# The feed-forward's hidden layer transposed as two planes of 16-bit words by a DMA instead of by TensorE

## The chip, the cores and the metric

The kernel runs on one core of a Trainium2 chip. The metric is the device time of one execution in microseconds; the kernel before takes 300.09 us (median of three runs, 300.06 to 302.69).

## The reference

One decoder layer over 256 tokens of width 1024, in float32: attention with 8 heads of 128, then a SwiGLU feed-forward of width 2816, each behind an RMS norm and with a residual add, and a last RMS norm. With 256 tokens there is one attention block, so the attention is plain causal attention. The part that the change touches is this:

```
def swiglu(h, w_in, w_out):
    g, u = jnp.split(jnp.einsum('bsd,df->bsf', h, w_in), 2, axis=-1)
    return jnp.einsum('bsf,fd->bsd', jax.nn.silu(g) * u, w_out)
```

## The kernel before, in words

All matrix products are made to nearly full float32 accuracy from three passes: a matrix is split into `hi` (cast to the format fp32r by ScalarE) and `lo` (what is left, by a subtract on VectorE), and `mm` (L93) issues hi x hi, hi x lo and lo x hi into one PSUM accumulator. So each 1 MB piece of weights that SP loads into a `raw` tile (four buffers) costs ScalarE a cast (L85) and VectorE a subtract (L86) per half, into `hi` and `lo` tiles (four buffers each).

The order on each engine comes from the Tile framework: it places instructions by its own priorities, keeps what depends on each other in order, and adds the waits. Buffers of a pool are reused in turn, so an instruction that writes a tile waits until the last reader of that buffer is done.

The feed-forward starts at L321. Its hidden layer is made in eleven chunks `c` of 256 hidden columns (gate and value, so 512 columns of `w_in`, in two pieces of 1 MB). `hidden(c)` issues 48 matmuls with 512 columns for the two tiles `t` of 128 tokens, then for each `t` a Silu on ScalarE (L348, tile `sg`) and a product on VectorE (L350), which leaves the chunk in `hs`, tokens on the partitions. The product with `w_out` needs the hidden index on the partitions. This turning is `turn(c)`: four TensorE transposes of 128x128 float32 against an identity into the PSUM tile `ph` (L366), and the split of `ph` into hi and lo by `split` (L354), which go to the large tiles named first, second and third. It is called for chunk c-1 after `hidden(c)`, so that TensorE meets the transposes between two chunks.

For the chunks in `SEVEN` (0, 2, 4, 6, 8) the 2x2 product of blocks with `w_out` is made with seven block products in place of eight. They need four sums of the blocks of `ph` (L377 to L380, tile `fs`) and sums of the rows of `w_out` (`load_out`, L390). To add two blocks that both lie in PSUM, one half of `ph` is first copied to the tile `fc` (L375).

The output stage then goes through the chunks 0 to 8: 21 matmuls for a chunk of SEVEN, 24 for another one. The last two chunks are kept for the end, where each output tile is finished, normed and stored. The turn of chunk 9 stands at the border of the two stages, and that of chunk 10 after the first chunk of the output stage:

```
            if c in SEVEN:
                seven_mm(c, wu[c])
                if c == 0:
                    turn(NC - 1, ph_last)
```

Of the kernel before, what the change touches and what calls it, by code (L numbers as in the profile page):

```python
# [25 lines left out]

F32 = mybir.dt.float32
F32R = mybir.dt.float32r
AF = mybir.ActivationFunctionType
ALU = mybir.AluOpType  # L30
AX = mybir.AxisListType

P = 128
T = 256
NT = T // P
# [5 lines left out]
NC = F // 256  # L41
# [7 lines left out]
SEVEN = (0, 2, 4, 6, 8)  # L49
# [5 lines left out]
def trunk(ctx, tc, xT, x, g2, g3, wv, wqk, wo, w_in, w_out, out):  # L55
    nc = tc.nc
# [8 lines left out]
    def held(n, dtype, slot):  # L65
        return home.tile([P, SLOTS[slot]], dtype, name=slot)[:, :n]

    wpool = ctx.enter_context(tc.tile_pool(name="wpool", bufs=4))
    small = ctx.enter_context(tc.tile_pool(name="small", bufs=2))
    ps_mm = ctx.enter_context(tc.tile_pool(name="ps_mm", bufs=4, space=PSUM))  # L70
    ps_a = ctx.enter_context(tc.tile_pool(name="ps_a", bufs=2, space=PSUM))
    ps_b = ctx.enter_context(tc.tile_pool(name="ps_b", bufs=2, space=PSUM))

    def weights():
        return [wpool.tile([P, 2048], d, name=n) for d, n in ((F32, "raw"), (F32R, "hi"), (F32R, "lo"))]

    def fetch(tiles, src, a, b, pieces=1, queue=nc.sync):

        raw, hi, lo = (w[:, a:b] for w in tiles)
        if queue is not None:  # L80
            queue.dma_start(raw, src[:, a:b])
        n = (b - a) // pieces
        for i in range(0, b - a, n):
            s = slice(i, i + n)
            nc.scalar.copy(hi[:, s], raw[:, s])  # L85
            nc.vector.tensor_sub(lo[:, s], raw[:, s], hi[:, s].bitcast(F32))  # L86

    def load(src, pieces=2):
        tiles = weights()
        fetch(tiles, src, 0, 2048, pieces)  # L90
        return tiles[1:]

    def mm(o, lh, ll, rh, rl, first, last):  # L93
        nc.tensor.matmul(o, lhsT=lh, rhs=rh, start=first, stop=False)  # L94
        nc.tensor.matmul(o, lhsT=lh, rhs=rl, start=False, stop=False)  # L95
        nc.tensor.matmul(o, lhsT=ll, rhs=rh, start=False, stop=last)  # L96
# [3 lines left out]
    ident = const.tile([P, P], F32, name="ident")  # L100
# [16 lines left out]
    nc.vector.memset(eps, EPS)  # L117
    nc.scalar.activation(scr[:, :1], eps, AF.Sqrt)
    pz = ps_b.tile([P, 512], F32, name="pb")
# [10 lines left out]
    def rstd_of(ss, name, bias=eps):  # L130
        r = small.tile([P, 1], F32, name=name)
        nc.scalar.activation(r, ss, AF.Sqrt, bias=bias, scale=1.0 / D)
        nc.vector.reciprocal(r, r)
        return r

    with tc.tile_pool(name="attn2", bufs=2) as a2:
        xh = const.tile([P, KD, T], F32R, name="xh")
        xl = const.tile([P, KD, T], F32R, name="xl")
        oh, ol = held(2 * H * T, F32R, "first").rearrange("p (i h t) -> i p h t", i=2, h=H)

# [6 lines left out]
        for k in range(KD):  # L147
# [5 lines left out]
            else:  # L153
                nc.scalar.activation(xh[:, k], xT_sb[:, k, :T], AF.Copy, scale=g)
            nc.vector.scalar_tensor_tensor(
# [10 lines left out]
            elif k - XK - 1 in range(NT):  # L166

                ss = small.tile([P, 1], F32, name="ss1")
                nc.scalar.activation(scr, x_sb[:, k - XK - 1], AF.Square, accum_out=ss)
                r1.append(rstd_of(ss, f"r1_{k}"))  # L170
        wk = {h: load(wqk[h]) for h in range(2)}

        pv = [[ps_mm.tile([P, 512], F32, name="pmm") for _ in range(2)] for _ in range(NT)]
# [13 lines left out]

        vh, vl = held(2 * D, F32R, "second").rearrange("p (i d) -> i p d", i=2)
        pr = ps_b.tile([P, T], F32, name="pb")
# [3 lines left out]
        for n in range(2):  # L193
            ns = slice(n * 512, (n + 1) * 512)
            nc.scalar.activation(vh[:, ns], pv[0][n], AF.Copy, scale=r1[0])
            nc.vector.scalar_tensor_tensor(
                vl[:, ns], pv[0][n], r1[0], vh[:, ns].bitcast(F32), op0=ALU.mult, op1=ALU.subtract
            )
            nc.scalar.activation(v1[:, ns], pv[1][n], AF.Copy, scale=r1[1])

        qk, pn, pt = {}, {}, {}

        def project(h):
# [10 lines left out]
            )  # L214
            fh = a2.tile([P, 3 * P], F32R, name="qkh")
            fl = a2.tile([P, 3 * P], F32R, name="qkl")
# [78 lines left out]
        r2, xg = [], {}  # L295

        def turn_x1(t, n):
            px = ps_b.tile([P, 4, P], F32, name="pb")
            for j in range(4):
                nc.tensor.transpose(px[:, j], xg[t, n][:, j * P : (j + 1) * P], ident)  # L300
            ks, ts = slice(4 * n, 4 * n + 4), slice(t * P, (t + 1) * P)
            nc.scalar.copy(x1h[:, ks, ts], px)
            nc.vector.tensor_sub(x1l[:, ks, ts], px, x1h[:, ks, ts].bitcast(F32))
# [19 lines left out]
    with tc.tile_pool(name="ffn2", bufs=2) as f2:  # L323
# [7 lines left out]

        hs_ = {}

        def hidden(c):
            u = [load(w_in[2 * c + i]) for i in range(2)]
            pf = [ps_mm.tile([P, 2, 256], F32, name="pmm") for _ in range(NT)]
            order = [(k, t) for k in range(KD) for t in range(NT)]
            if c == 0:
                order.sort(key=lambda kt: kt[1])
            for k, t in order:  # L340
                if c == 0 and (k, t) == (0, 1):
                    turn_x1(1, 1)
                wh, wl = (w.rearrange("p (k n) -> p k n", k=4)[:, k % 4] for w in u[k // 4])
                ts = slice(t * P, (t + 1) * P)
                mm(pf[t].rearrange("p a b -> p (a b)"), x1h[:, k, ts], x1l[:, k, ts], wh, wl, k == 0, k == KD - 1)
            for t in range(NT):
                sg = f2.tile([P, 256], F32, name="sg")
                nc.scalar.activation(sg, pf[t][:, 0], AF.Silu, scale=r2[t])  # L348
                hs_[c, t] = f2.tile([P, 256], F32, name="hs", bufs=4)
                nc.vector.scalar_tensor_tensor(  # L350
                    hs_[c, t], pf[t][:, 1], r2[t], sg, op0=ALU.mult, op1=ALU.mult
                )

        def split(at, src):  # L354

            to = parts(at, at + int(np.prod(src.shape[1:])))
            h, l = (t.rearrange("p (a b) -> p a b", a=src.shape[1]) for t in to)
            nc.scalar.copy(h, src)
            nc.vector.tensor_sub(l, src, h.bitcast(F32))

        def turn(c, ph=None):
            if ph is None:
                ph = ps_a.tile([P, 2, T], F32, name="pa")
            for j in range(2):
                for t in range(NT):
                    nc.tensor.transpose(ph[:, j, t * P : (t + 1) * P], hs_[c, t][:, j * P : (j + 1) * P], ident)  # L366
            if c not in SEVEN:
                split(HAT[c], ph)
                return
            a11, a21, a12, a22 = (ph[:, j, t * P : (t + 1) * P] for j in range(2) for t in range(NT))  # L370
            split(HAT[c], ph[:, 0:1, :P])
            split(HAT[c] + P, ph[:, 1:2])
            fs = f2.tile([P, 4, P], F32, name="fs")
            fc = f2.tile([P, 2, P], F32, name="fc")
            nc.scalar.copy(fc, ph[:, :, P:])  # L375

            nc.vector.tensor_sub(fs[:, 0], a21, fc[:, 1])  # L377
            nc.vector.tensor_add(fs[:, 1], a11, fc[:, 0])
            nc.vector.scalar_tensor_tensor(fs[:, 2], fs[:, 0], -1.0, a11, op0=ALU.mult, op1=ALU.subtract)
            nc.vector.tensor_add(fs[:, 3], a12, fs[:, 2])  # L380
            split(HAT[c] + 3 * P, fs)

        for c in range(NC):
            hidden(c)
            if c > 0:
                turn(c - 1)

# [26 lines left out]
        def bank(pool, n=512):  # L416
            return pool.tile([P, n], F32, name="pmm" if pool is ps_mm else "pb" if pool is ps_b else "pa")


        ph_last = ps_a.tile([P, 2, T], F32, name="pa")  # L420
        acc7 = {i: bank(p) for i, p in ((2, ps_b), (1, ps_b), (3, ps_mm), (7, ps_mm), (5, ps_a), (6, ps_mm), (4, ps_mm))}

        SIDES = {2: (1, 0, 0), 1: (0, 0, 1), 3: (6, 0, 2), 7: (4, 2, 1), 5: (3, 2, 0), 6: (5, 2, 2), 4: (2, 2, 3)}
# [12 lines left out]
                mm(o, *parts(at, at + P), ws[0][:, e], ws[1][:, e], first and j == 0, last and j == 1)  # L436

        TAIL = NC - 2
        wu = {}
        for c in range(TAIL):  # L440
            wu[c] = load_out(c)
            if c in SEVEN:
                seven_mm(c, wu[c])
                if c == 0:
                    turn(NC - 1, ph_last)
                    corners = {(0, 0): acc7[2], (0, 512): acc7[3], (1, 0): acc7[4], (1, 512): bank(ps_a)}
            else:
                for (t, a), o in corners.items():
                    eight_mm(c, wu[c], t, a, 512, o, (t, a) == (1, 512) and c == 1)
        for c in range(TAIL, NC):  # L450
            wu[c] = load_out(c)
# [27 lines left out]
        for i, (t, o, (a, b), (ra, rb)) in enumerate(plan):  # L479
            for c in range(TAIL, NC):  # L480
                eight_mm(c, wu[c], t, a, b - a, o[:, : b - a], o is last and c == TAIL, c == NC - 1)

# [76 lines left out]
```

## Time and profile before

| | |
|---|---|
| median of three runs | 300.09 us (300.06 to 302.69) |
| the profiled execution's own time | 299.56 us |
| span of its trace, first to last instruction | 297.8 us |
| TensorE matmul busy | 290.2 us, 97% |
| VectorE, ScalarE busy | 210.9 us (71%), 167.9 us (56%) |
| transposes of L366 | 44, 272 ns each |
| mean granted TensorE clock | 0.996 |

Matmuls are pipelined: the next one starts before the one ahead has ended, and the ends are modelled. So durations of matmuls cannot be added; the distance from start to start is what one costs on the path. The names PE, PEld, DVE, ACT and SP stand for TensorE, its weight load, VectorE, ScalarE and SyncE; SPq is SP's queue of DMA issues.

### The profile page before, as it was taken

What the parts mean: (1) busy time and instruction counts of PE and PEld (TensorE: products, weight loads), DVE (VectorE), ACT (ScalarE), POOL (GpSimd) and SP (SyncE); (2) the same over time, 40 slices, a digit from 0 to 9 for tenths busy, and PEclk for the clock granted to TensorE, in tenths of its full rate; (3) what the DMA queues carried; (4) which work ended last, traced back from release to release, by engine and by line L of the source; (5) the groups of instructions that cost most, each with busy time, mean ns of one, the idle gap of its engine ahead of it and who ended that gap; (6) DMA issues with size and microseconds to landing.
All of it is one profiled execution on the core that took longest, in us unless ns stands there. A gap on an engine that the chain in (4) does not pass through costs nothing.

```text
span 297.8 us, 4015 instructions
## 1 busy us (share of the span) xinstructions
PE 290.2 (97%) x1544; PEld 247.6 (83%) x1544; DVE 210.9 (71%) x328; ACT 167.9 (56%) x272; POOL 1.3 (0%) x8
## 2 busy tenths in 40 slices
PE   7999999999999999999999999999999999999992
PEld 4788999999988888888888888888888888888881
DVE  4756988777776587657647647749857698888684
ACT  4786886555555496555455446446426647445443
POOL 1000000000000000000000000000000000000000
PEclk9999999999999999999999999999999999999998
DMA  6999895644445406764365465352333444670003
GB/s 200 383 411 418 289 351 194 236 146 151 142 156 190 165 36 222 281 261 155 141 241 183 143 227 196 141 196 88 141 144 119 163 158 145 262 252 31 2 0 141
DMA packets 10099, 55.84 MB, mean 188 GB/s; under 512 B 1120, under 2 KB 2656, under 8 KB 4192
## 3 DMA queue, kind: packets, MB, share of 16 engines
q1 hardware_dynamic: 9648, 55.06, 50.7%
q10 hardware_dynamic: 432, 0.52, 0.5%
q8 instruction: 12, 0.20, 0.3%
q14 instruction: 7, 0.06, 0.1%
HBM read 54.53 MB, written 1.05 MB: 187 GB/s over the span
## 4 chain that ended last, share of the span: by engine, by line
PE 94%; DMA 2%; DVE 1%; ACT 1%; SPq 1%; issue 0%
PE pmm L96 23%; PE pmm L94 23%; PE pmm L95 23%; PE pmm L179 7%; PE pb L96 2%; PE pb L94 2%; PE pb L95 2%; PE pa L94 2%; PE pa L96 2%; PE pa L95 2%; DMA raw<-in_wv 2%; PE pa L366 2%; PE pa L245 1%; PE pb L224 1%; PE pb L260 1%; PE pb L300 1%
## 5 line engine op out<-in xcount | busy, mean ns | idle before, releaser
L86 DVE TENSOR_TENSOR lo<-raw,hi 128x1024 fp32r<-128x1024 f32 (+2 forms) x91 | 106.4, 1185 | 38.9 <-ACT hi L85 38.6
L85 ACT CAST hi<-raw 128x1024 fp32r<-128x1024 f32 (+2 forms) x91 | 90.8, 1021 | 50.1 <-PE pmm L96 23.7
L94 PE MATMUL pmm<-hi,xh 128*128 128x512 f32 x176 | 69.6, 396 | 0.0
L96 PE MATMUL pmm<-hi,xl 128*128 128x512 f32 x176 | 68.7, 390 | 0.0
L95 PE MATMUL pmm<-lo,xh 128*128 128x512 f32 x176 | 68.5, 389 | 0.0
L96 PEld LDWEIGHTS pmm<-hi,xl 128*128 128x128 f32 x176 | 33.0, 188 | 7.1
L95 PEld LDWEIGHTS pmm<-lo,xh 128*128 128x128 f32 x176 | 33.1, 188 | 6.6
L94 PEld LDWEIGHTS pmm<-hi,xh 128*128 128x128 f32 x176 | 33.0, 188 | 6.5
L94 PE MATMUL pmm<-hi,first 128*128 128x512 f32 x76 | 30.3, 398 | 0.0
L95 PE MATMUL pmm<-lo,first 128*128 128x512 f32 x76 | 29.6, 389 | 0.0
L94 PE MATMUL pmm<-xh,hi 128*128 128x256 f32 x96 | 27.6, 287 | 0.0
L96 PE MATMUL pmm<-xh,lo 128*128 128x256 f32 x96 | 27.1, 283 | 0.0
L95 PE MATMUL pmm<-xl,hi 128*128 128x256 f32 x96 | 27.1, 283 | 0.0
L348 ACT ACTIVATE sg<-pmm,r 128x256 f32<-128x256 f32 x22 | 10.4, 475 | 28.8 <-PE pmm L96 28.6
L399 ACT CAST hi<-raw 128x1024 fp32r<-128x1024 f32 (+1 forms) x15 | 17.5, 1193 | 14.9 <-issue 6.6
L400 DVE TENSOR_TENSOR lo<-raw,hi 128x1024 fp32r<-128x1024 f32 (+1 forms) x15 | 20.4, 1398 | 6.2 <-ACT hi L399 6.1
L350 DVE SCALAR_TENSOR_TENSOR hs<-pmm,r,sg 128x256 f32<-128x256 f32 x22 | 10.6, 483 | 14.9 <-ACT sg L348 14.9
L95 PEld LDWEIGHTS pmm<-xl,hi 128*128 128x128 f32 x96 | 18.4, 192 | 0.0
L96 PEld LDWEIGHTS pmm<-xh,lo 128*128 128x128 f32 x96 | 18.4, 191 | 0.0
L94 PEld LDWEIGHTS pmm<-xh,hi 128*128 128x128 f32 x96 | 18.4, 191 | 0.0
L95 PEld LDWEIGHTS pmm<-lo,first 128*128 128x128 f32 x76 | 14.3, 188 | 2.8
L94 PEld LDWEIGHTS pmm<-hi,first 128*128 128x128 f32 x76 | 14.3, 188 | 2.7
(143 smaller groups left out, 425.5 us busy)
## 6 DMA issues: line engine op xcount, KB each, us to landing
raw<-in_w_in SPq DMA_DIRECT2D x22, 1024.0 KB, 4.8
raw<-in_w_out SPq DMA_DIRECT2D x11, 1024.0 KB, 4.8
raw<-in_wqk SPq DMA_DIRECT2D x8, 1024.0 KB, 7.4
raw<-in_wo SPq DMA_DIRECT2D x4, 1024.0 KB, 4.8
raw<-in_wv SPq DMA_DIRECT2D x7, 512.0 KB, 7.7
second<-in_xT SPq DMA_DIRECT2D x8, 128.5 KB, 6.8
x_sb<-in_x SPq DMA_DIRECT2D x1, 1024.0 KB, 9.5
g_bc<-in_g SPq DMA_DIRECT2D x2, 512.0 KB, 5.5
```

Source lines behind the costliest of these rows:

```text
L85: nc.scalar.copy(hi[:, s], raw[:, s])
L86: nc.vector.tensor_sub(lo[:, s], raw[:, s], hi[:, s].bitcast(F32))
L94: nc.tensor.matmul(o, lhsT=lh, rhs=rh, start=first, stop=False)
L95: nc.tensor.matmul(o, lhsT=lh, rhs=rl, start=False, stop=False)
L96: nc.tensor.matmul(o, lhsT=ll, rhs=rh, start=False, stop=last)
L179: nc.tensor.matmul(pv[t][a // 512][:, a % 512 : a % 512 + b - a], lhsT=l[:, k, t * P : (t + 1) * P], rhs=r[:, a:b],  start=k == 0 and a % ...
L224: nc.tensor.matmul(ps[:, :P], lhsT=f[:, :P], rhs=f[:, T : T + P], start=True, stop=True)
L348: nc.scalar.activation(sg, pf[t][:, 0], AF.Silu, scale=r2[t])
L350: nc.vector.scalar_tensor_tensor(hs_[c, t], pf[t][:, 1], r2[t], sg, op0=ALU.mult, op1=ALU.mult)
L366: nc.tensor.transpose(ph[:, j, t * P : (t + 1) * P], hs_[c, t][:, j * P : (j + 1) * P], ident)
L399: nc.scalar.copy(h[:, a:b], r[:, a:b])
L400: nc.vector.tensor_sub(l[:, a:b], r[:, a:b], h[:, a:b].bitcast(F32))
```

## The change

`hs` becomes one tile per chunk, one buffer, with the two 128-column halves, the token tiles and the columns as its axes. `turn(c)` no longer uses TensorE. ScalarE copies `hs`, read as 16-bit words, into a tile `planes`: first all words of one half of the float32 bits, then all of the other (1024 elements in all on a partition). One DMA on SP's queue, `dma_start_transpose`, writes the eight 128x128 blocks of 16-bit words turned into `turned` (two buffers). A new function `join(c)` puts the words together again: a ScalarE copy writes them into `ph`, now a float32 tile in SBUF, and the split and the four sums follow as before, with `ph` as their source. With `ph` in SBUF the copy `fc` goes. `join(c-2)` is called after `turn(c-1)`, so one chunk later than the turn. The loads of `w_in` are now requested one chunk ahead in the program (`early`, `ahead`).

```diff
--- before.py
+++ after.py
@@ -26,6 +26,7 @@
 
 F32 = mybir.dt.float32
 F32R = mybir.dt.float32r
+U16 = mybir.dt.uint16
 AF = mybir.ActivationFunctionType
 ALU = mybir.AluOpType
 AX = mybir.AxisListType
@@ -85,10 +86,17 @@
             nc.scalar.copy(hi[:, s], raw[:, s])
             nc.vector.tensor_sub(lo[:, s], raw[:, s], hi[:, s].bitcast(F32))
 
-    def load(src, pieces=2):
-        tiles = weights()
-        fetch(tiles, src, 0, 2048, pieces)
+    def load(src, pieces=2, raw=None):
+        tiles = [wpool.tile([P, 2048], F32, name="raw") if raw is None else raw]
+        tiles += [wpool.tile([P, 2048], F32R, name=n) for n in ("hi", "lo")]
+        fetch(tiles, src, 0, 2048, pieces, queue=nc.sync if raw is None else None)
         return tiles[1:]
+
+    def early(src):
+
+        raw = wpool.tile([P, 2048], F32, name="raw")
+        nc.sync.dma_start(raw, src)
+        return raw
 
     def mm(o, lh, ll, rh, rl, first, last):
         nc.tensor.matmul(o, lhsT=lh, rhs=rh, start=first, stop=False)
@@ -331,8 +339,10 @@
 
         hs_ = {}
 
+        ahead = {i: early(w_in[i]) for i in range(2)}
+
         def hidden(c):
-            u = [load(w_in[2 * c + i]) for i in range(2)]
+            u = [load(w_in[i], raw=ahead.pop(i)) for i in (2 * c, 2 * c + 1)]
             pf = [ps_mm.tile([P, 2, 256], F32, name="pmm") for _ in range(NT)]
             order = [(k, t) for k in range(KD) for t in range(NT)]
             if c == 0:
@@ -343,12 +353,17 @@
                 wh, wl = (w.rearrange("p (k n) -> p k n", k=4)[:, k % 4] for w in u[k // 4])
                 ts = slice(t * P, (t + 1) * P)
                 mm(pf[t].rearrange("p a b -> p (a b)"), x1h[:, k, ts], x1l[:, k, ts], wh, wl, k == 0, k == KD - 1)
+            hs_[c] = f2.tile([P, 2, NT, P], F32, name="hs", bufs=1)
             for t in range(NT):
                 sg = f2.tile([P, 256], F32, name="sg")
                 nc.scalar.activation(sg, pf[t][:, 0], AF.Silu, scale=r2[t])
-                hs_[c, t] = f2.tile([P, 256], F32, name="hs", bufs=4)
                 nc.vector.scalar_tensor_tensor(
-                    hs_[c, t], pf[t][:, 1], r2[t], sg, op0=ALU.mult, op1=ALU.mult
+                    hs_[c][:, :, t],
+                    pf[t][:, 1].rearrange("p (j f) -> p j f", j=2),
+                    r2[t],
+                    sg.rearrange("p (j f) -> p j f", j=2),
+                    op0=ALU.mult,
+                    op1=ALU.mult,
                 )
 
         def split(at, src):
@@ -358,32 +373,51 @@
             nc.scalar.copy(h, src)
             nc.vector.tensor_sub(l, src, h.bitcast(F32))
 
-        def turn(c, ph=None):
-            if ph is None:
-                ph = ps_a.tile([P, 2, T], F32, name="pa")
-            for j in range(2):
-                for t in range(NT):
-                    nc.tensor.transpose(ph[:, j, t * P : (t + 1) * P], hs_[c, t][:, j * P : (j + 1) * P], ident)
+        turned_ = {}
+
+        def turn(c):
+
+
+            planes = f2.tile([P, 2, 4 * P], U16, name="planes", bufs=1)
+            nc.scalar.copy(planes, hs_[c].bitcast(U16).rearrange("p j t (f w) -> p w (j t f)", w=2))
+            turned = f2.tile([P, 2, 4 * P], U16, name="turned")
+            turned_[c] = turned
+            nc.sync.dma_start_transpose(
+                turned.rearrange("p w (b t) -> p (w b) t", b=4), planes.rearrange("p w n -> p (w n)")
+            )
+
+        def join(c):
+
+            turned = turned_.pop(c)
+            ph = f2.tile([P, 2, T], F32, name="ph", bufs=1)
+
+            tc.keep_in_program_order(
+                nc.scalar.copy(
+                    ph.bitcast(U16).rearrange("p j (t w) -> p (j t) w", w=2), turned.rearrange("p w n -> p n w")
+                )
+            )
             if c not in SEVEN:
                 split(HAT[c], ph)
                 return
             a11, a21, a12, a22 = (ph[:, j, t * P : (t + 1) * P] for j in range(2) for t in range(NT))
             split(HAT[c], ph[:, 0:1, :P])
             split(HAT[c] + P, ph[:, 1:2])
-            fs = f2.tile([P, 4, P], F32, name="fs")
-            fc = f2.tile([P, 2, P], F32, name="fc")
-            nc.scalar.copy(fc, ph[:, :, P:])
-
-            nc.vector.tensor_sub(fs[:, 0], a21, fc[:, 1])
-            nc.vector.tensor_add(fs[:, 1], a11, fc[:, 0])
+            fs = f2.tile([P, 4, P], F32, name="fs", bufs=1)
+
+            nc.vector.tensor_sub(fs[:, 0], a21, a22)
+            nc.vector.tensor_add(fs[:, 1], a11, a21)
             nc.vector.scalar_tensor_tensor(fs[:, 2], fs[:, 0], -1.0, a11, op0=ALU.mult, op1=ALU.subtract)
             nc.vector.tensor_add(fs[:, 3], a12, fs[:, 2])
             split(HAT[c] + 3 * P, fs)
 
         for c in range(NC):
+            for i in range(2 * c + 2, min(2 * c + 4, 2 * NC)):
+                ahead[i] = early(w_in[i])
             hidden(c)
             if c > 0:
                 turn(c - 1)
+            if c > 1:
+                join(c - 2)
 
 
 
@@ -417,7 +451,6 @@
             return pool.tile([P, n], F32, name="pmm" if pool is ps_mm else "pb" if pool is ps_b else "pa")
 
 
-        ph_last = ps_a.tile([P, 2, T], F32, name="pa")
         acc7 = {i: bank(p) for i, p in ((2, ps_b), (1, ps_b), (3, ps_mm), (7, ps_mm), (5, ps_a), (6, ps_mm), (4, ps_mm))}
 
         SIDES = {2: (1, 0, 0), 1: (0, 0, 1), 3: (6, 0, 2), 7: (4, 2, 1), 5: (3, 2, 0), 6: (5, 2, 2), 4: (2, 2, 3)}
@@ -436,15 +469,19 @@
                 mm(o, *parts(at, at + P), ws[0][:, e], ws[1][:, e], first and j == 0, last and j == 1)
 
         TAIL = NC - 2
+        PLAIN = [c for c in range(TAIL) if c not in SEVEN]
         wu = {}
         for c in range(TAIL):
             wu[c] = load_out(c)
             if c in SEVEN:
                 seven_mm(c, wu[c])
                 if c == 0:
-                    turn(NC - 1, ph_last)
+                    turn(NC - 1)
+                    join(NC - 2)
                     corners = {(0, 0): acc7[2], (0, 512): acc7[3], (1, 0): acc7[4], (1, 512): bank(ps_a)}
             else:
+                if c == PLAIN[0]:
+                    join(NC - 1)
                 for (t, a), o in corners.items():
                     eight_mm(c, wu[c], t, a, 512, o, (t, a) == (1, 512) and c == 1)
         for c in range(TAIL, NC):
```

The first place is TensorE between hidden chunks 2 and 3, around the turn of chunk 1. Before:

```order
L95 MATMUL pmm<-lo,xh 128x512
L96 MATMUL pmm<-hi,xl 128x512
L366 MATMUL pa<-ident,hs 128x128 [waits DVE_49] x2
L366 MATMUL pa<-ident,hs 128x128 x2
L94 MATMUL pmm<-hi,xh 128x512 [waits Activation_49]
L95 MATMUL pmm<-lo,xh 128x512
L96 MATMUL pmm<-hi,xl 128x512
```

Now, the same place:

```order
L103 MATMUL pmm<-lo,xh 128x512
L104 MATMUL pmm<-hi,xl 128x512
L102 MATMUL pmm<-hi,xh 128x512 [waits DVE_49]
L103 MATMUL pmm<-lo,xh 128x512
L104 MATMUL pmm<-hi,xl 128x512
```

The four transposes are gone; the matmuls around them stand as they stood (lines 94 to 96 are now 102 to 104). This holds at all eleven places.

The second place is ScalarE's queue from the Silus of chunk 3 to the last cast before those of chunk 4. Before, with the turn of chunk 2:

```order
L348 ACTIVATE sg<-pmm,r_0_1193 128x256 [waits DVE_49,PE_49]
L348 ACTIVATE sg<-pmm,r_1_1239 128x256 [waits DVE_49,PE_49]
L85 CAST hi<-raw 128x1024 [waits DMAHW4_49]
L358 CAST first<-pa 128x128 [waits PE_49]
L85 CAST hi<-raw 128x1024
L358 CAST first<-pa 128x256 [waits DVE_49]
L375 COPY fc<-pa 128x256 [waits DVE_49]
L85 CAST hi<-raw 128x1024 [waits DMAHW5_49,PE_49]
L358 CAST first<-fs 128x512 [waits DVE_49]
L85 CAST hi<-raw 128x1024
```

Now, with the planes of chunk 3 and the join of chunk 2:

```order
L359 ACTIVATE sg<-pmm,r_0_1193 128x256 [waits PE_49]
L359 ACTIVATE sg<-pmm,r_1_1239 128x256 [waits PE_49]
L86 CAST hi<-raw 128x1024 [waits DMAHW6_49]
L382 COPY planes<-hs 128x1024 [waits DMAHW0_49,DVE_49]
L395 COPY ph<-turned 128x1024 [waits Activation_49]
L86 CAST hi<-raw 128x1024
L373 CAST first<-ph 128x128 [waits Activation_49]
L373 CAST first<-ph 128x256
L373 CAST first<-fs 128x512 [waits DVE_49]
L86 CAST hi<-raw 128x1024 [waits DMAHW7_49,PE_49]
L86 CAST hi<-raw 128x1024
```

The two copies stand between the first and the second cast after the Silus. The planes copy waits for the DMA of the chunk before (its semaphore is DMAHW0 here) and for VectorE's product; the join behind it reads what that DMA wrote. The copy fc is gone, and the cast of fs has moved ahead of a weight cast.

The third place is the turnover to the output stage. On SP, before, the loads of `w_out` chunks 1 to 5:

```order
L81 DMA raw<-in_w_out 128x2048 [waits DMAHW5_49,DVE_49]
L396 DMA raw<-in_w_out 128x2048 [waits DMAHW6_49,DVE_49]
L81 DMA raw<-in_w_out 128x2048 [waits DMAHW4_49,DVE_49]
L396 DMA raw<-in_w_out 128x2048 [waits DMAHW0_49,DVE_49]
L81 DMA raw<-in_w_out 128x2048 [waits DMAHW7_49,DVE_49]
```

Now, from the load of chunk 2 to that of chunk 6, with the transposes of hidden chunks 9 and 10 (line 385):

```order
L430 DMA raw<-in_w_out 128x2048 [waits DMAHW5_49,DMAHW2_49,DVE_49]
L385 DMA_TRANSPOSE turned<-planes 128x8x128 [waits DMAHW7_49,Activation_49]
L82 DMA raw<-in_w_out 128x2048 [waits DVE_49]
L430 DMA raw<-in_w_out 128x2048 [waits DMAHW0_49,DVE_49]
L385 DMA_TRANSPOSE turned<-planes 128x8x128 [waits DMAHW6_49,DMAHW1_49,Activation_49]
L82 DMA raw<-in_w_out 128x2048 [waits DVE_49]
L430 DMA raw<-in_w_out 128x2048 [waits DMAHW4_49,DVE_49]
```

On ScalarE now, from the last Silu of the hidden stage to the first casts of `w_out` chunk 4 (L433 with 1536 is the first cast of a seven-product chunk, L86 casts the chunks between):

```order
L359 ACTIVATE sg<-pmm,r_1_1239 128x256 [waits PE_49]
L433 CAST hi<-raw 128x1536 [waits DMAHW2_49]
L382 COPY planes<-hs 128x1024 [waits DMAHW3_49,DVE_49]
L395 COPY ph<-turned 128x1024 [waits Activation_49]
L433 CAST hi<-raw 128x1024 [waits PE_49]
L373 CAST first<-ph 128x512 [waits Activation_49]
L433 CAST hi<-raw 128x1024
L86 CAST hi<-raw 128x1024 [waits DMAHW4_49,PE_49]
L395 COPY ph<-turned 128x1024 [waits DMAHW6_49,DVE_49]
L86 CAST hi<-raw 128x1024
L373 CAST first<-ph 128x512 [waits Activation_49]
L433 CAST hi<-raw 128x1536 [waits DMAHW5_49,PE_49]
```

The transpose of chunk 10 is issued behind the loads of `w_out` chunks 3 and 4. Its join stands in ScalarE's queue between the two casts of chunk 3. Planes and join of the chunks before stand between the casts of chunk 2. On VectorE the wide add of `w_out` chunk 4 (L438, L404 before) now stands ahead of the second subtract of chunk 2; before, it stood behind the subtracts of chunk 3.

## Rows read from the trace of the kernel before

**Rows 1.** The page: busy us of each engine, share of the span, count of instructions.

```profile
PE 290.2 (97%) x1544; PEld 247.6 (83%) x1544; DVE 210.9 (71%) x328; ACT 167.9 (56%) x272; POOL 1.3 (0%) x8
```

**Rows 2.** The page: the chain that ended last, by engine.

```profile
PE 94%; DMA 2%; DVE 1%; ACT 1%; SPq 1%; issue 0%
```

**Rows 3.** Waits of TensorE: us in total, times, longest us.

```profile
PE pb L121 <- DVE eps L117: 1.2, 1, 1.2
PE pmm L179 <- ACT hi L85: 0.5, 2, 0.3
```

**Rows 4.** Line 366: duration ns min/median/max, first and last start us.

```profile
L366 PE MATMUL pa<-ident,hs x44: 272/272/273, 131.9 to 239.8; 128*128 128x128 f32 x44
```

**Rows 5.** The chain in order of time, 154 to 167: start us, us, what.

```profile
154.81 0.44 PE pa L366 x4
...
166.18 0.44 PE pa L366 x4
```

**Rows 6.** Time line, 154 to 168: start us, us, engine, line, operation, tiles.

```profile
154.42 0.39 PE L96 MATMUL pmm<-hi,xl 128*128 128x512 f32 x1
...
154.65 0.60 PE L366 MATMUL pa<-ident,hs 128*128 128x128 f32 x4
...
155.22 1.04 ACT L85 CAST hi<-raw 128x1024 fp32r<-128x1024 f32 x1
155.32 0.40 PE L95 MATMUL pmm<-lo,xh 128*128 128x512 f32 x1
...
155.35 0.48 DVE L350 SCALAR_TENSOR_TENSOR hs<-pmm,r,sg 128x256 f32<-128x256 f32 x1 [0.20 <-ACT sg L348]
...
156.16 0.27 ACT L358 CAST first<-pa 128x128 fp32r<-128x128 f32 x1
...
157.17 0.39 PE L94 MATMUL pmm<-hi,xh 128*128 128x512 f32 x1
...
165.34 0.39 PE L94 MATMUL pmm<-hi,xh 128*128 128x512 f32 x1
```

**Rows 7.** Windows: us, busy us (x instructions) PE, PEld, DVE, ACT, POOL; clock, DMA share, GB/s.

```profile
154.80:166.20 11.40, 11.40 (x55) 9.43 (x53) 7.76 (x14) 6.27 (x10) 0.00 (x0) 1.00 0.51 178
166.20:177.60 11.40, 11.40 (x54) 9.43 (x53) 6.38 (x8) 5.34 (x8) 0.00 (x0) 1.00 0.57 195
```

**Rows 8.** ScalarE, 120 to 234, by line and form: busy us, mean ns; idle before.

```profile
L85 ACT CAST hi<-raw 128x1024 fp32r<-128x1024 f32 x37 | 38.3, 1051 | 18.0 <-PE pmm L96 18.0
...
L358 ACT CAST first<-pa 128x256 fp32r<-128x256 f32 x5 | 1.9, 374 | 1.9 <-DVE second L359 1.1 <-DVE third L359 0.8
L375 ACT COPY fc<-pa 128x256 f32<-128x256 f32 x5 | 1.9, 373 | 5.5 <-DVE second L359 3.3 <-DVE third L359 2.2
...
L358 ACT CAST first<-pa 128x128 fp32r<-128x128 f32 x5 | 1.3, 266 | 0.0
```

**Rows 9.** Waits of ScalarE: us in total, times, longest us.

```profile
ACT sg L348 <- PE pmm L96: 28.6, 21, 3.3
ACT hi L85 <- PE pmm L96: 23.7, 12, 3.1
```

**Rows 10.** DMA issues: KB each, median us from issue to landing.

```profile
raw<-in_w_in SPq DMA_DIRECT2D x22, 1024.0 KB, 4.8
...
x_sb<-in_x SPq DMA_DIRECT2D x1, 1024.0 KB, 9.5
...
out_y<-xh SPq DMA_DIRECT2D x2, 320.0 KB, 2.5
...
raw<-in_wv SPq DMA_DIRECT2D x1, 256.0 KB, 3.8
```

**Rows 11.** Time line, 233 to 246, of SP, VectorE and TensorE.

```profile
233.09 0.33 SPq L396 DMA_DIRECT2D raw<-in_w_out  x1
...
238.67 2.35 DVE L400 TENSOR_TENSOR lo<-raw,hi 128x1024 fp32r<-128x1024 f32 x2
...
245.44 0.39 PE L94 MATMUL pb<-hi,first 128*128 128x512 f32 x1
```

## Prediction

> **What bounds the kernel now.** I read the page from the top. TensorE is busy for 290.2 of 297.8 us, ScalarE for 167.9 and VectorE for 210.9 [rows 1]. The chain that ended last is 94% TensorE [rows 2], and in the list of waits TensorE stands with two entries only, 1.2 and 0.5 us, at the idle matmuls of the start and at the value projection, neither in the feed-forward [rows 3]. So between about 8 and 289 us every TensorE instruction stands on the path that sets the end: what is taken off that queue comes off the time, as long as nothing else is then late. The granted clock is 1.00 in the stretches I asked for, the 2.4 GHz level [rows 7].
>
> **What the change takes off TensorE.** The 44 transposes of line 366, eleven groups of four [rows 4]. Their 272 ns each overlap, so the price has to be read from the path. The chain gives a group 0.44 us, and repeats it every 11.37 us [rows 5]. The time line gives it a second way: from the start of the last matmul before a group (154.42) to the start of the second after it (155.32) is 0.90 us, and two matmuls at the pitch of the same chunk, (165.34 - 157.17) / 36 = 0.227 us, would take 0.454 [rows 6]. The difference is 0.446 us. Eleven times: **4.9 us**. The order on TensorE is otherwise the same, row for row.
>
> **What it adds, and what hides it.** Per hidden chunk there are now two ScalarE copies (planes, join), one DMA from SP, and a few operations that change their source.
>
> *ScalarE.* The trace has no copy of 16-bit words. The nearest row by count of elements is the cast of 128x1024, SBUF to SBUF, 1.05 us [rows 8]. Half of that (0.5, if bytes set it) and double (2.1, if the 4-byte step costs) are my ends; I take 1.05, since the rows of 128 and 256 elements (0.27, 0.37) grow with the elements. ScalarE is busy 6.27 and 5.34 us in two neighbouring chunks of 11.4 us [rows 7]. Two copies add 2.1 and, in a seven-product chunk, the 0.37 us copy fc goes: 8.0 and 7.4 of the new period of 11.37 - 0.44 = 10.93 us. At 2.1 us a copy it would be 10.1 and 9.5, still under the period. At nothing, then. The cover is the time in which ScalarE waits for TensorE, 28.6 us before the Silu and 23.7 before the casts [rows 9]. Where that is gone, TensorE waits for weights or for its PSUM banks.
>
> *VectorE.* It keeps its operation count: the subtracts and the four sums now read ph in SBUF. VectorE is busy 7.76 us in a seven-product chunk [rows 7]. At nothing.
>
> *The weights.* The two copies push the second cast after the Silu, and with it the release of the raw buffer and the next issue on SP, back by some 2 us. Such a load lands 4.8 us after issue [rows 10], and with four raw buffers it isn't cast until two chunks on. Nothing.
>
> *The DMA transpose* moves 256 KB and stands on the SP queue ahead of two loads that wait for VectorE anyway. Its price is in no row. The nearest in size and row length is the 256 KB load of wv, 3.8 us to landing; the ends are the shortest landing of the trace, 2.5 us for 320 KB, and the longest among those rows, 9.5 us for 1 MB in the crowd of the first loads [rows 10]. I take 3.8. What hides it: the next planes copy has to wait for it (one planes buffer), and so does the join behind it. In the time line the Silu is followed by a cast that starts at 155.22, and the next instruction at 156.16 [rows 6]; planes takes that place, 156.2 to 157.2. The next planes copy comes one period on, at 167.1. So the transfer has **9.9 us**, and both ends fit.
>
> A rule of the Trainium skill speaks against the change: VectorE: DVE Perf Modes, The three transpose paths, gives 1309 ns for a 128x128 transpose of 16-bit words on the DMA path against 390 on TensorE, and advises TensorE where the result may lie in PSUM, as here. Eight such blocks one behind the other would be an estimated 10.5 us, just over the cover. Against it, DMA: Bandwidth & Descriptors (Latency and other measured facts) gives 261 GB/s for a DMA transpose, an estimated 1.0 us for 256 KB. The trace agrees with the first only in that TensorE's price is small; by either figure the sum stays at 4.9 us or within a microsecond of it.
>
> *The turnover to w_out.* Here weights are ready with the least lead: the second part of the third w_out chunk is finished on VectorE at 241.0 (238.67 + 2.35) and its matmuls start at 245.44 [rows 11]. In the new order planes and join stand between the Silu and those casts (2.1 us), and VectorE does the wide add of the fifth chunk first (1.2 us). 241.0 + 3.3 = 244.3, against 245.44 - 0.44 = 245.0: 0.7 us to spare. The last transpose is issued at about 237.5, behind a 1 MB load that SP issues near 233.1 [rows 11] and that lands by 237.9; it is there by some 241.5, when ScalarE reaches the join. At 9.5 us the join would hold the casts of the fourth chunk until 248 and these would be done at about 249.4, near the moment they are needed (245.44 + 21 x 0.227 - 0.44 = 249.8). Nothing, but tight. The last transposed chunks are used only at the very end.
>
> **The sum.** Against the profiled execution, 299.56 us for a span of 297.8: 299.56 - 4.9 = 294.7. That execution lies 0.5 below the median of the runs, 300.09; from the median the same sum is **295.2 us**.
>
> **Rivals.**
> 1. *The transfer sets the pace (slower).* If the eight blocks of a transpose go one behind the other, each at a price of its own, landing takes longer than 9.9 us, and planes of chunk c+1 waits for the transpose of chunk c. A period is then landing + 1.05 us. TensorE has a cover of some 10 us in all, since the PSUM banks that it needs after the next group of transposes (166.2) were drained at 155.8 [rows 5, 6]. Over ten periods the loss is 10 x (landing - 9.9) - 10: it eats the gain from a landing of 11.4 us on. Eight times the shortest landing, 2.5 us, is 20 us; the time would be 295.2 + 91 = 386. For it: nothing in the trace shows how blocks run together. Against it: 1 MB, four times the size of a transpose, lands in 4.8 us [rows 10]. By the figure of 1309 ns in the Trainium skill (the page above) the loss would be under the cover and the time 295 to 296. Chance 0.10, with other mishaps on that side.
> 2. *A part is lost at the turnover.* With copies of 2.1 us the third w_out chunk is ready at 246.4 in place of 245.0, and VectorE carries the lag on: TensorE waits 1 to 3 us, 296.2 to 298. For it: the 0.7 us to spare. Against it: VectorE has idle time there that my sum ignores. Chance 0.10.
> 3. *No change.* TensorE only looks full, and preparing the weights on ScalarE and VectorE sets the period: TensorE would wait for what it no longer transposes, 300.1. For it: VectorE is 71% busy overall. Against it: ScalarE waits for TensorE before every Silu, and chunks with 7.76 and 6.38 us of VectorE take the same 11.4 us [rows 7]. Chance 0.05. That the change doesn't do what it says is excluded by the order: 44 matmuls are gone, eleven transposes stand on SP.
>
> **How the numbers follow.** The forecast has 0.75 and by itself lies between 294.0 and 296.2: 4.9 us, the 0.5 us between the two times of before, and a little of the turnover. The range of 8 in 10 reaches up into the second rival, 298.0; left out are the third, the first and the tails. One per cent, about what a measurement of this kernel tells from no change, is 3.0 us: faster is below 297.1. That holds the forecast and some 0.06 of the second rival: 0.81. Within 1%: the rest of it and the third, 0.09. Slower: 0.10.
>
> **What would show it.** Right: TensorE with 44 matmuls fewer, a period of 10.93 us between Silus, no new TensorE wait, the transposes landing in under 9.9 us, planes and join at about 1.05 us. Wrong: ScalarE waiting at planes or join for the DMA transpose, with TensorE idle before the first matmul of a chunk on VectorE or ScalarE (first rival); TensorE idle at the third or fourth w_out chunk (second); a period of 11.4 us with TensorE waits on lo (third).

## The result, and the profile after

The changed kernel takes 294.85 us (median of four runs, 294.5 to 295.3) against 300.14 us before: a ratio of 0.9823 with an interval of 0.980 to 0.9846, 5.3 us less. The forecast was 295.2 us.

The page of the changed kernel, its line of engines, its chain by engine and its DMA lines:

```profile
PE 284.3 (97%) x1500; PEld 243.5 (83%) x1500; DVE 210.6 (72%) x328; ACT 188.1 (64%) x289; POOL 1.3 (0%) x8
...
DMA packets 21715, 58.72 MB, mean 200 GB/s; under 512 B 12736, under 2 KB 14272, under 8 KB 15808
...
q1 hardware_dynamic: 21264, 57.94, 57.4%
...
PE 94%; DMA 2%; DVE 1%; ACT 1%; SPq 1%; issue 0%
```

TensorE has 44 instructions fewer than in [rows 1] and is still busy for 97% of a shorter span; ScalarE has 20 us more, and the share of the chain is that of [rows 2]. The work went from the engine that sets the end to one that doesn't.

TensorE's whole list of waits in the changed kernel (us in total, times, longest):

```profile
PE pmm L187 <- ACT hi L86: 1.8, 3, 1.3
PE pb L129 <- DVE eps L125: 1.2, 1, 1.2
```

As in [rows 3], nothing in the feed-forward. The entry at L187, the value projection, is longer by 1.3 us: there the first weights come later in this execution, as below.

The time line of the changed kernel on TensorE, at the border of two chunks, where [rows 6] had the transposes:

```profile
154.59 0.39 PE L103 MATMUL pmm<-lo,xh 128*128 128x512 f32 x1
154.82 0.39 PE L104 MATMUL pmm<-hi,xl 128*128 128x512 f32 x1
155.05 0.39 PE L102 MATMUL pmm<-hi,xh 128*128 128x512 f32 x1
155.28 0.39 PE L103 MATMUL pmm<-lo,xh 128*128 128x512 f32 x1
155.50 0.39 PE L104 MATMUL pmm<-hi,xl 128*128 128x512 f32 x1
```

Starts are 0.227 us apart with no break. The same stretch on ScalarE:

```profile
154.57 0.47 ACT L359 ACTIVATE sg<-pmm,r 128x256 f32<-128x256 f32 x1 [0.20 <-PE pmm L104]
154.94 1.04 ACT L86 CAST hi<-raw 128x1024 fp32r<-128x1024 f32 x1
155.88 1.05 ACT L382 COPY planes<-hs 128x1024 uint16<-128x1024 uint16 x1
156.82 1.17 ACT L395 COPY ph<-turned 128x1024 uint16<-128x1024 uint16 x1
157.90 1.05 ACT L86 CAST hi<-raw 128x1024 fp32r<-128x1024 f32 x1
...
164.77 0.47 ACT L359 ACTIVATE sg<-pmm,r 128x256 f32<-128x256 f32 x1 [2.75 <-PE pmm L104]
165.45 0.47 ACT L359 ACTIVATE sg<-pmm,r 128x256 f32<-128x256 f32 x1 [0.20 <-PE pmm L104]
```

From the second Silu of one chunk to that of the next it is 165.45 - 154.57 = 10.88 us, where [rows 5] had 11.37. No idle time stands before planes or join, so the DMA was in; the idle time is still before the Silu, 2.75 us of it, and it is TensorE that ends it. Two windows of one such period each, with the columns of [rows 7]:

```profile
154.57:165.45 10.88, 10.88 (x49) 9.01 (x48) 7.75 (x14) 7.89 (x12) 0.00 (x0) 1.00 0.67 218
165.45:176.33 10.88, 10.88 (x49) 9.01 (x48) 6.38 (x8) 7.38 (x10) 0.00 (x0) 1.00 0.73 220
```

ScalarE is busy for 7.89 and 7.38 us (8.0 and 7.4 were worked out), VectorE as before. The DMA transpose and the copy that reads it, by line, with the time from issue to landing:

```profile
L385 SPq DMA_TRANSPOSE turned<-planes x11: 1237/1239/2148, 124.3 to 233.5; - x11
...
L395 ACT COPY ph<-turned x11: 1166/1169/1172, 135.1 to 237.9; 128x1024 uint16<-128x1024 uint16 x11
...
DMA to landing us min/median/max: 3.0/3.1/4.3
```

The median landing is 3.1 us, under the 3.8 that was taken, and far under the cover.

The profiled execution of the changed kernel took 295.0 us, 4.56 less than the one before, not 5.3. The rest is at the start: the first weights landed 1.0 us later in it. The chain of the changed kernel, then of the kernel before:

```profile
2.59 6.24 DMA raw<-in_wv
```

```profile
2.58 5.24 DMA raw<-in_wv
```

The first matmul of the hidden stage starts at 110.27 us in place of 109.54, 0.73 late. With that put back, 4.56 + 0.73 = 5.29, the difference of the medians.

### The profile page after: what moved, and what is told of

It is laid out like the page before. It is cut to its first block, busy times and chain, and to the rows that moved or that the text cites. A ratio compares the mean times of both kernels' runs of the same rounds, so it can differ in the third digit from the quotient of the medians.

```text
span 293.1 us, 3958 instructions
## 1 busy us (share of the span) xinstructions
PE 284.3 (97%) x1500; PEld 243.5 (83%) x1500; DVE 210.6 (72%) x328; ACT 188.1 (64%) x289; POOL 1.3 (0%) x8
## 3 DMA queue, kind: packets, MB, share of 16 engines
q1 hardware_dynamic: 21264, 57.94, 57.4%
HBM read 54.53 MB, written 1.05 MB: 190 GB/s over the span
## 4 chain that ended last, share of the span: by engine, by line
PE 94%; DMA 2%; DVE 1%; ACT 1%; SPq 1%; issue 0%
PE pmm L104 23%; PE pmm L103 23%; PE pmm L102 23%; PE pmm L187 7%; PE pb L104 2%; PE pb L102 2%; PE pb L103 2%; PE pa L103 2%; PE pa L102 2%; PE pa L104 2%; DMA raw<-in_wv 2%; PE pa L253 1%; PE pb L232 1%; PE pb L268 1%; PE pb L308 1%; DVE x_sb L522 1%
## 5 line engine op out<-in xcount | busy, mean ns | idle before, releaser
L86 ACT CAST hi<-raw 128x1024 fp32r<-128x1024 f32 (+2 forms) x91 | 90.3, 1020 | 35.5 <-PE pmm L103 13.6
L102 PE MATMUL pmm<-hi,xh 128*128 128x512 f32 x176 | 68.7, 390 | 0.0
L433 ACT CAST hi<-raw 128x1024 fp32r<-128x1024 f32 (+1 forms) x15 | 17.6, 1193 | 9.4 <-issue 6.9
L360 DVE SCALAR_TENSOR_TENSOR hs<-pmm,r,sg 128x256 f32<-128x256 f32 x22 | 10.5, 483 | 15.2 <-ACT sg L359 15.2
L103 PEld LDWEIGHTS pmm<-xl,hi 128*128 128x128 f32 x96 | 18.4, 192 | 0.0
L102 PEld LDWEIGHTS pmm<-xh,hi 128*128 128x128 f32 x96 | 18.4, 191 | 0.0
L104 PEld LDWEIGHTS pmm<-xh,lo 128*128 128x128 f32 x96 | 18.4, 191 | 0.0
```

The source lines that it names most:

```text
L360: nc.vector.scalar_tensor_tensor(hs_[c][:, :, t], pf[t][:, 1].rearrange("p (j f) -> p j f", j=2), r2[t], sg.rearrange("p (j f) -> p j f", ...
L433: nc.scalar.copy(h[:, a:b], r[:, a:b])
```

## The experiments

All were run beside the kernel before, which took 299.8 to 300.0 us there.

**The transposes put back on TensorE** (`e1_pe4`), with all else of the change kept:

```diff
+            extra = ps_a.tile([P, 2, T], F32, name="pa")
+            for i in range(4):
+                j, t = i // 2 % 2, i % 2
+                nc.tensor.transpose(extra[:, j, t * P : (t + 1) * P], ident, ident)
             planes = f2.tile([P, 2, 4 * P], U16, name="planes", bufs=1)
```

> The changed kernel with four TensorE transposes of the identity per chunk put back at the eleven places (their result is not used). My theory, that the whole gain is TensorE path time: the period between Silus goes back from 10.88 to 11.37 us and the time to 294.85 + 11 x 0.49 = 300.2 (299.7 to 300.7). Rival, that the gain comes from the loads asked for one chunk earlier or from the new order on ScalarE and VectorE: the time stays nearer 295 to 297.

Measured: 299.99 us (299.64 to 300.3), ratio to before 1.000 (0.9988 to 1.0012). The whole gain is gone, with the loads, nearly the whole order and the DMA of the change in place. The rival is out.

**Eight in place of four** (`e2_pe8`, `range(8)`):

> The same with eight transposes per place. It parts the price of the transposes themselves from the price of breaking the run of matmuls. If each costs the 0.109 us of the chain and the rest of 0.49 us is paid once per place: 300.2 + 11 x 0.436 = 305.0. If the whole 0.49 goes with the count: 305.6. Rival as before: far below 305.

Measured: 304.84 us (304.28 to 305.27), as for the price paid once per break. The chain of `e1_pe4`, then of `e2_pe8`:

```profile
144.12 0.44 PE pa L384 x4
155.47 0.44 PE pa L384 x4
166.81 0.44 PE pa L384 x4
```

```profile
144.44 0.88 PE pa L384 x8
156.22 0.87 PE pa L384 x8
168.01 0.87 PE pa L384 x8
```

A chunk takes 11.35 us with four, 11.79 with eight and 10.88 with none: the second four cost 0.44, the first four 0.47.

**The loads alone** (`e3_loads`): the kernel before with `early` and `ahead` of the change, nothing else.

> The kernel before with nothing changed but the loads of w_in asked for one chunk ahead in the program. My theory: the weights were never late, so 300.1 (299.6 to 300.6). Rival, that the earlier requests carry a part of the gain: 295 to 299.

Measured: 300.03 us (299.71 to 300.19), ratio 0.9996 (0.9984 to 1.0009). Asking earlier for weights that are never late brings nothing.

**No turning at all** (`e4_no_turn`). It leaves the turning out, so it doesn't compute the layer; it only shows what the added work costs. `hs` gets three buffers in place of one, since it is now read later:

```diff
-            hs_[c] = f2.tile([P, 2, NT, P], F32, name="hs", bufs=1)
+            hs_[c] = f2.tile([P, 2, NT, P], F32, name="hs", bufs=3)
...
         def turn(c):
-            planes = f2.tile([P, 2, 4 * P], U16, name="planes", bufs=1)
...
+            turned_[c] = hs_[c]
         def join(c):
-            ph = f2.tile([P, 2, T], F32, name="ph", bufs=1)
...
+            ph = turned.rearrange("p j t f -> p j (t f)")
```

> The changed kernel without planes copy, DMA transpose and join: the split reads hs unturned, so this leaves the turning out altogether. My theory, that all of what was added is hidden: 294.9 (294.4 to 295.4), no faster than the changed kernel. Rival, that a part of the added work is on the path: 292 to 294.

Measured: 294.56 us median (294.46 to 296.49), ratio to before 0.9829 (0.9789 to 0.9869), against 0.9823 for the changed kernel. Twenty-two copies and eleven DMAs less, and no time less than such a measurement can tell.

**The DMA made longer** (`e5_serial3`, `e5_serial4`), the transpose issued three and four times; each waits for the one ahead, since all write the same tile:

```diff
-            nc.sync.dma_start_transpose(
...
+            for _ in range(3):
+                nc.sync.dma_start_transpose(
...
```

> The changed kernel with each DMA transpose issued three times, one after the other's landing (same source, same result). My theory: the cover is 9.9 us; three landings of 3.1 us make 9.3, so the time stays at 294.9 (294.4 to 296). Rival, that the transfer already stands near the path (for example because the loads behind it on SP come late): 300 or more.

> The same with four in a row. My theory: 12.4 us are over the cover of 9.9; ScalarE waits at the planes copy, a chunk takes 12.4 + 1.05 = 13.45 us in place of 10.88, ten chunks lose 25.7 us, of which a cover of about 10 us is taken off: 294.9 + 15.7 = 310.6 (305 to 321). Rival, that TensorE can run on far ahead of the turning and the transfers only have to be in by the end: below 300.

Measured: 310.69 us (309.98 to 313.4) and 334.47 us (330.58 to 335.12). Both expectations missed. The rival put to the first, 300 or more, came out in its number, but not by loads that come late: TensorE waits 0.6 us for weights there. The waits of `e5_serial3` show the mechanism of the first rival, ScalarE waiting for the transpose at planes; the line of TensorE shows where it is paid, at the product on VectorE that must drain its PSUM banks. Three of these five waits, 3.8 us, lie in the hidden stage; the other two, 10.1 us, at the first matmuls of the output stage:

```profile
ACT planes L382 <- DMA turned<-planes: 48.9, 9, 7.5
```

```profile
PE pmm L102 <- DVE hs L360: 14.0, 5, 8.3
```

What was wrong is the length. SP's queue and the next planes copy in `e5_serial3`:

```profile
166.95 5.41 SPq L386 DMA_TRANSPOSE turned<-planes  x2
172.46 0.52 SPq L98 DMA_DIRECT2D raw<-in_w_in  x1
174.20 1.24 SPq L386 DMA_TRANSPOSE turned<-planes  x1
```

```profile
179.19 1.05 ACT L382 COPY planes<-hs 128x1024 uint16<-128x1024 uint16 x1 [5.64 <-DMA turned<-planes]
```

The three transposes landed 4.2, 3.1 and 4.9 us after their issues, and the whole took 179.19 - 166.95 = 12.2 us, not 9.3. The third was issued 1.7 us after a 1 MB load, which itself landed after 5.6 us in place of the usual 4.8 [rows 10]. The first came 4.6 us behind another load, issued at 162.31. That loads and transposes held each other up is the likely reading; no run separates them. The ten distances between planes copies, from the first and last starts (kernel after, then with three, then with four):

```profile
L382 ACT COPY planes<-hs x11: 1037/1047/1050, 123.2 to 232.5; 128x1024 uint16<-128x1024 uint16 x11
```

```profile
L382 ACT COPY planes<-hs x11: 1040/1047/1048, 122.9 to 256.5; 128x1024 uint16<-128x1024 uint16 x11
```

```profile
L382 ACT COPY planes<-hs x11: 1037/1046/1047, 122.7 to 292.1; 128x1024 uint16<-128x1024 uint16 x11
```

That is 10.9, 13.4 and 16.9 us a chunk. With 13.4 the formula of the prediction gives a loss of 10 x (13.4 - 10.9) - 10 = 15.0 us. TensorE's waits in this trace, 14.0 us on the product and 0.6 on lo, come to 14.6: the cover of some 10 us is there.

The traced execution took 313.4 us, though, 18.4 more than that of the changed kernel (295.0), so 3.8 us more than the waits. The formula has no term for what comes behind a long wait. TensorE's first matmuls after the longest one, and the window of their stretch with the columns of [rows 7]:

```profile
250.16 0.80 PE L102 MATMUL pmm<-hi,first 128*128 128x512 f32 x1 [8.26 <-DVE hs L360]
250.75 0.63 PE L103 MATMUL pmm<-lo,first 128*128 128x512 f32 x1
251.17 0.63 PE L104 MATMUL pmm<-hi,second 128*128 128x512 f32 x1
...
255.00 0.40 PE L104 MATMUL pb<-hi,second 128*128 128x512 f32 x1
```

```profile
250.10:255.00 4.90, 4.84 (x12) 3.84 (x12) 4.33 (x5) 3.92 (x5) 0.00 (x0) 0.50 0.89 247
```

They start 0.43 us apart in place of 0.227, and the granted clock is 0.50, the 1.2 GHz level. The eleven from 250.16 to 255.00 take 4.8 us in place of 2.5, which is 2.3 of the 3.8 us.

With 16.9 the formula gives a loss of 50 us, and that of the traced execution is 334.3 - 295.0 = 39.3. Here more was changed than the DMA: the framework also put TensorE's instructions in another order. In its time line 66 matmuls of the output stage stand ahead of the last wait for a product, where `e5_serial3` and the changed kernel have 15. That is an estimated 51 x 0.227 = 11.6 us of cover more, the size of what the formula is off by. So `e5_serial4` tests the formula only together with this estimate.

**The copies made longer** (`e6_copies2`, `e6_copies3`), each of planes and join two and three times:

```diff
-            nc.scalar.copy(planes, hs_[c].bitcast(U16).rearrange("p j t (f w) -> p w (j t f)", w=2))
+            for _ in range(2):
+                nc.scalar.copy(planes, hs_[c].bitcast(U16).rearrange("p j t (f w) -> p w (j t f)", w=2))
...
```

> The changed kernel with the planes copy and the join copy each made twice: 2.0 us more on ScalarE per chunk, the upper end of the price in the prediction. My theory: ScalarE waits 2.75 us before each pair of Silus, so it still fits: 294.9 (294.4 to 295.6). Rival 2 of the prediction, that a part is lost at the turnover to the output stage with copies of this length: 296 to 298, with TensorE idle at the third or fourth chunk of w_out.

> The same with each copy three times: 4.0 us more. ScalarE's idle time of a chunk (2.75 us after a seven-product chunk, 3.3 after another) is used up and 0.7 to 1.3 us are missing, about 10 us over the ten chunks. My theory: TensorE's cover of about 10 us takes most of it, and the lag is paid at the turnover: 296 to 302, with TensorE waiting for lo or hi of w_out and not in the hidden stage. Rival, that there is no such cover: about 305; rival, that ScalarE's time doesn't matter: 294.9.

Measured: 294.61 us (294.0 to 295.06) and 296.74 us (296.3 to 296.94). With double copies ScalarE's wait before the Silus shrinks and nothing else happens; the second rival of the prediction is out. With triple copies the 1.9 us lie at the low end of what was expected. They are paid at the turnover, as expected, but TensorE doesn't wait there for lo or hi of w_out: its first matmuls of the output stage wait for PSUM banks that VectorE's last products must drain. The list of waits, then the time line:

```profile
PE pmm L102 <- DVE hs L360: 1.6, 2, 1.1
```

```profile
234.82 0.50 PE L102 MATMUL pmm<-hi,first 128*128 128x512 f32 x1 [1.07 <-DVE hs L360]
...
236.28 0.50 PE L102 MATMUL pmm<-hi,first 128*128 128x512 f32 x1 [0.48 <-DVE hs L360]
```

**The join at once** (`e7_join_soon`):

```diff
             if c > 0:
                 turn(c - 1)
-            if c > 1:
-                join(c - 2)
+                join(c - 1)
...
```

> The changed kernel with the join of a chunk called right after its turn in place of one chunk later. ScalarE then waits for the DMA inside the chunk: landing 3.1 us less the one cast between, some 2.2 us on top of the 7.9 and 7.4 us that it is busy, 10.1 and 9.6 of a period of 10.88. My theory, that only landing within ScalarE's idle time matters: 294.9 (294.3 to 296). Rival, that the delay by a chunk is what hides the transfer: 297 to 305, with TensorE waiting for hs or lo.

Measured: 294.91 us (294.86 to 295.15), ratio 0.983 (0.9814 to 0.9847). ScalarE does wait, and it costs nothing:

```profile
ACT ph L395 <- DMA turned<-planes: 25.0, 10, 3.6
```

So the chunk of delay that the change gives the DMA isn't what hides it: ScalarE's idle time alone is enough for 3 to 4 us.

**The attention's weights by DMA too** (`e8_p_by_dma`): `transpose_p` becomes `turn_p` (planes copy and DMA) and `join_p`, in dead parts of the head's tile.

```diff
-            for step, i in ((attend, h - 3), (scores, h - 1), (transpose_p, h - 2)):
+            for step, i in ((attend, h - 4), (join_p, h - 3), (scores, h - 1), (turn_p, h - 2)):
```

> The changed kernel with the softmax weights of the attention also turned by DMA: the 24 transposes in eight groups of three go from TensorE, planes and turned words lie in dead parts of the head's own tile, and each head is attended one step later. A group costs 0.33 us on the chain and by e1_pe4 and e2_pe8 some 0.04 for the break: 8 x 0.37 = 3.0 us. ScalarE is busy 4.09 of 7.25 us per head and gets 1.7 us more. My theory: 291.9 (291.3 to 293). Rival, that the later step makes TensorE wait at the end of the attention, where the last heads are attended just ahead of their use: 293 to 296.

Measured: 294.19 us median of five, 293.07 to 295.7; 291.3 to 293 was expected. The scores' matmuls of two heads, in the changed kernel, then here:

```profile
68.60 0.39 PE L232 MATMUL pb<-qk 128*128 128x128 f32 x2
75.85 0.39 PE L232 MATMUL pb<-qk 128*128 128x128 f32 x2
```

```profile
67.21 0.39 PE L232 MATMUL pb<-qk 128*128 128x128 f32 x2
74.13 0.39 PE L232 MATMUL pb<-qk 128*128 128x128 f32 x2
```

A head takes 6.92 us in place of 7.25, so the price of three transposes is 0.33, without the break that was added to it. The times lie too far apart for a verdict, so it was run again beside the changed kernel (`e9_p_again`, `e10_change_again`).

> The kernel of e8_p_by_dma once more, side by side with the changed kernel: its five times lay between 293.1 and 295.7, too wide to say whether it is faster than the changed kernel. By its trace (6.92 us per head in place of 7.25, the feed-forward reached 2.0 us earlier) my theory: 2 us under the changed kernel, 292.9 (292 to 294). Rival, that in some executions the loads of the attention and the transposes delay each other on the one queue: the times spread over 2 us again, with a median within 1 us of the changed kernel.

> The changed kernel itself on the same chip, for the comparison: 294.85 (294.4 to 295.4) by its earlier runs, a spread under 1 us.

Measured: four of six times at 292.46 to 293.08 and two at 296.46 and 297.08, median 292.85, ratio to before 0.9784 (0.9744 to 0.9823); the changed kernel 294.87 (294.17 to 295.1), ratio 0.9829 (0.9814 to 0.9844). So four of six times it is 1.8 to 2.4 us faster than the changed kernel, but two of six times it was slower, and the intervals just overlap with 0.9823 and 0.9814: whether it is faster is open. What happens in the long executions isn't known: the profiled ones were short and show no TensorE wait in the attention. Of the four longest executions of this kernel three have a mean granted clock of 0.989 to 0.991 and one 0.998, the others 0.993 to 0.999, so a lower clock goes with most of them, not with all.

## Why the prediction was right, point by point

*What bounds.* Right. Putting four transposes back (`e1_pe4`) takes the gain away to within 0.1 us of the kernel before, and leaving out the copies and the DMA that replaced them (`e4_no_turn`) brings nothing that can be told from noise. The path through TensorE is the whole story, and the loads are no part of it (`e3_loads`).

*The price of the transposes.* The mechanism was right, the size a little low: 0.446 us a group was read over two matmuls, 11.37 - 10.88 = 0.49 is what a chunk lost. The matmuls behind a group keep a pitch of 0.231 us in [rows 6] (157.17 - 155.32 over eight), where the changed kernel has 0.227: 8 x 0.0045 = 0.036 of the missing 0.044. Eleven times 0.49 is 5.4, and 5.3 was measured. A step that breaks a run of matmuls is best priced from period to period.

*ScalarE.* Right: planes 1.05 us as taken, join 0.12 longer at 1.17; the upper end of the range was free too, as `e6_copies2` showed.

*The DMA.* Right that it is hidden. Its landing, 3.1 us, lay inside the range and under the value taken. The Trainium skill (VectorE: DVE Perf Modes, The three transpose paths) gives 1309 ns for one 128x128 block on the DMA path. The prediction's estimate of eight such blocks one behind the other, 10.5 us, isn't what the trace shows: eight blocks in one instruction land in 3.1 us. The advice to take TensorE where the result may lie in PSUM stands on the same page of the Trainium skill under Rules for kernel authors. It doesn't hold here: TensorE's transpose is the cheaper one, some 0.12 us each (0.49 / 4), but it stands on the path, and the DMA's doesn't.

*The turnover.* Pessimistic. The second part of the third w_out chunk is done on VectorE at 237.31 + 1.22 = 238.5 in the changed kernel, TensorE reaches it at 240.73, and the last transpose, issued at 233.54, has landed by 236.6, before its join starts at 237.86:

```profile
233.54 1.24 SPq L385 DMA_TRANSPOSE turned<-planes  x1
```

```profile
237.31 1.22 DVE L434 TENSOR_TENSOR lo<-raw,hi 128x1024 fp32r<-128x1024 f32 x1
```

```profile
240.73 0.39 PE L102 MATMUL pb<-hi,first 128*128 128x512 f32 x1
```

That leaves 2.2 us, not 0.7, and two terms of the sum were off. It had put ScalarE's copies and VectorE's add one behind the other, 3.3 us; they lie side by side, and VectorE is done 7.3 us after the start of the last product in place of 6.0, so 1.3 later. And it took one group of transposes, 0.44 us, off TensorE's way to this chunk, where in the kernel before two stood behind the last matmul of the hidden stage:

```profile
234.26 0.60 PE L366 MATMUL pa<-ident,hs 128*128 128x128 f32 x4
...
239.51 0.60 PE L366 MATMUL pa<-ident,hs 128*128 128x128 f32 x4
```

*The first rival.* Its mechanism is real, and the cover in its formula about right: in `e5_serial3` ScalarE stops at planes, and TensorE waits 14.6 us where the formula gives 15.0. Where it tips, by the prediction at a landing of 11.4 us, no run brackets: 3.1 us is hidden, some 12 is not. It lacked two things. The landing is not the transpose's alone, since loads on the same queue come in between; and behind its longest wait in `e5_serial3` TensorE ran at the lower clock, which cost 2.3 us.

## What to carry to other kernels

Where one engine is on the path all the time, price a step there by the change of its period, and moving it to idle engines is worth that price even if they take ten times as long over it (1.05 + 3.1 + 1.17 = 5.3 us here, for 0.49). Work out the cover of what is moved (here 9.9 us for a transfer that lands in 3.1, and some 5 us of ScalarE's idle time a chunk for 2.2 us of copies) and then stretch it in an experiment until it tears. A transfer's landing beside few other loads is no measure of it among many on its queue.

## What the runs showed of the hardware that was not expected

A DMA transpose of 256 KB adds 1056 packets: the queue has 21264 packets where the kernel before had 9648, 11616 more for eleven, and the count of packets under 512 B grows by the same 11616. For its bytes it holds the DMA engines long. The queue's line on the page of the kernel before (packets, MB, share of sixteen engines' span), which answers to that of the changed kernel above:

```profile
q1 hardware_dynamic: 9648, 55.06, 50.7%
```

That is 0.507 x 16 x 297.8 = 2416 engine-us before, and 0.574 x 16 x 293.1 = 2692 now: 276 more for eleven transposes, 25 each if the loads held the engines as long as before. Per MB these take 276 / (57.94 - 55.06) = 96 engine-us, and all that was there before 2416 / 55.06 = 44. This fits transposes and loads that delay each other, as `e5_serial3` suggests; no run separates the two.

A ScalarE copy of 1024 16-bit words with a step of two words takes 1.05 us, as long as the cast of 1024 float32: the time goes with the count of elements here, not with the bytes. Reading from two planes in turn (join) takes 1.17.
